# Moving the last residual load of a streaming RMSNorm into SyncE's queue, between the last x groups

## The chip, the cores and the metric

One NeuronCore of a Trainium2 chip. The metric is device time in microseconds; fast means within 1.5% of the quickest run of the same kernel. Repeated runs of one kernel agree within about half a microsecond to one and a half, at most 1.8 us (nine runs of the kernel before in one job). A profiled span is some 1.8 us shorter than the timed run that it comes from, so spans are compared with spans and times with times.

## The reference

```python
# x, residual: (32, 2048, 2048) float32; gamma: (2048,); eps = 1e-6
z = x + residual
rms = np.sqrt(np.mean(z ** 2, axis=-1, keepdims=True) + eps)
return (z / rms * gamma).astype(np.float32)
```

65,536 rows of 2048 numbers are read twice (x and residual) and written once: 1.61 GB.

## The kernel before

Rows are cut into 65 tiles, 0 to 64. Tile 0 has three rows in each of 128 partitions, tile 64 five, the others eight. Two z buffers take x and become the output in place; one residual buffer `r_area` of nine rows is shared by neighbouring tiles, shifted so that the next residual can be loaded as soon as the first part of the tile before has been added. VectorE adds and scales, ScalarE squares and takes roots, SyncE issues x and the stores, ScalarE issues the residuals.

```python
def sp_turn(sp, i):                       # SyncE, tile i
    def load(q):                          # a quarter of the partitions of tile i+1
        sp.wait_ge(s_out[q], i * U)       # the same quarter of tile i-1 is stored
        load_x(sp, i + 1, q)
    Turn(i).wait(sp, "done", -1)          # tile i-1 is scaled
    for q in range(Q):                    # Q = 4
        store(sp, i - 1, q)
    for q in range(Q):
        load(q)
...
def act_turn(s, t, chain):                # ScalarE, tile i
    ...
    t.wait(s, "add_a")                    # first part of the tile is added
    squares(s, chain, z[p], a, m, ssq[p][0], 0)
    if i == last - 1:
        load_r(s, t, 1)                   # the last residual, on ScalarE's queue
    elif i:
        t.wait(s, "add_b")
        load_r(s, t, 1)
    ...
# SyncE after its turns: tile 63 in two stores, tile 64 in three (2, 2 and 1 rows)
sp.wait_ge(half, 1);                 store_rows(sp, last - 1, a0, b0)
Turn(last).wait(sp, "done", -1);     store_rows(sp, last - 1, a1, b1)
for k, (a, b) in enumerate(tail):
    sp.wait_ge(tail_ev["done"], k + 1)
    store_rows(sp, last, a, b)
```

Of the kernel before, what the change touches and what calls it, by code (L numbers as in the profile page):

```python
# [9 lines left out]
def kernel(  # L10
# [32 lines left out]
    Q = 4  # L43
# [9 lines left out]
    last = n_tiles - 1  # L53
# [6 lines left out]
    def rows(t, i):  # L60
        k = sizes[i]
        return t[starts[i] : starts[i] + P * k, :].rearrange("(p r) m -> p r m", r=k)
# [45 lines left out]
    def res(i, a, b):  # L108

        if i == 0:  # L110
            return z[0][:, 5 + a : 5 + b, :]
        e = 4 if i == last else 0 if i % 2 else 1
        return r_area[:, e + a : e + b, :]

    def parts(i):

        if i == 0:
            return [(0, 1), (1, 2), (2, 3)]
        return [(4, R), (1, 4), (0, 1)] if i % 2 else [(0, 4), (4, R - 1), (R - 1, R)]
# [21 lines left out]
    def inc(ins, kind, i):  # L141
        return ins.then_inc(ev[kind][i % 2], U)
# [5 lines left out]
    def load_x(sp, i, q):  # L148
        sp.dma_start(out=z[i % 2][group(q), : sizes[i], :], in_=rows(x_f, i)[group(q)]).then_inc(
            ev["x_in"][i % 2], U  # L150
        )
# [6 lines left out]
    def load_r(eng, t, d=0):  # L158
        i = t.i + d
        inc(  # L160
            eng.dma_start(  # L161
                out=res(i, 0, sizes[i]),
                in_=rows(r_f, i) if t.it is None else r_full[t.it + (i - 1)],
            ),
            "r_in",
            i,
        )

    def store(sp, i, q):
        sp.dma_start(out=rows(o_f, i)[group(q)], in_=z[i % 2][group(q), : sizes[i], :]).then_inc(  # L170
            s_out[q], U
        )
# [4 lines left out]
    def sp_turn(sp, i):  # L177


        def load(q):  # L180
            sp.wait_ge(s_out[q], i * U)
            load_x(sp, i + 1, q)

        Turn(i).wait(sp, "done", -1)
        for q in range(Q):
            store(sp, i - 1, q)
        for q in range(Q):
            load(q)


# [48 lines left out]
    def squares(s, chain, src, a, b, sq, c):  # L239

        for g in range(a, b):
            chain.wait()
            chain.next(
                s.activation(  # L244
                    out=sq_junk[:, :],
                    in_=src[:, g, :],
                    func=Act.Square,
                    accum_out=sq[:, c + g - a : c + g - a + 1],
                )
            )  # L250

    def root(s, chain, sq, rm):
        chain.wait()
        return s.activation(out=rm, in_=sq, func=Act.Sqrt, bias=eps_tile[:, :], scale=inv_d)  # L254

    def act_turn(s, t, chain):
        i, p = t.i, t.p
        (a, b), (a1, b1), (a2, b2) = parts(i)
        m = b - 1 if i else b
        t.wait(s, "add_a")  # L260
        squares(s, chain, z[p], a, m, ssq[p][0], 0)
        if i == last - 1:

            load_r(s, t, 1)
        elif i:
            t.wait(s, "add_b")
            load_r(s, t, 1)
        squares(s, chain, z[p], m, b, ssq[p][0], m - a)
        n = b - a
        inc(root(s, chain, ssq[p][0][:, :n], rms[p][0][:, :n]), "rms_a", i)  # L270
        c = min(a1, a2)
        n = b1 - a1 + b2 - a2
        if i == 0 or i == last - 1:
            t.wait(s, "add_b")
        squares(s, chain, z[p], a1, b1, ssq[p][1], a1 - c)
        t.wait(s, "add_c")
        squares(s, chain, z[p], a2, b2, ssq[p][1], a2 - c)
        inc(root(s, chain, ssq[p][1][:, :n], rms[p][1][:, :n]), "rms_b", i)
# [5 lines left out]
    def sync_program(sp):  # L284
        whole_x(sp, 0)
        load_r(sp, Turn(0))

        sp.wait_ge(tail_ev["add"], 1)
        for q in range(4):
            sp.dma_start(  # L290
                out=stage[32 * q : 32 * q + 1],
                in_=gamma.partition_broadcast(1).rearrange("p (a b) -> p a b", a=16),
            ).then_inc(g_in, U)
        load_r(sp, Turn(1))
        whole_x(sp, 1)
        for i in range(1, last):
            sp_turn(sp, i)
        (a0, b0), (a1, b1) = halves(last - 1)
        sp.wait_ge(half, 1)
        store_rows(sp, last - 1, a0, b0)  # L300
        Turn(last).wait(sp, "done", -1)
        store_rows(sp, last - 1, a1, b1)
# [3 lines that stand above are left out]
# [30 lines left out]
    def scalar_program(s):  # L336
        chain = Chain(s, act)
        for i in range(LO):
            act_turn(s, Turn(i), chain)
        with s.Fori(0, 2 * (n_iter - 1), 2) as it:  # L340
            n = chain.n
            chain.base = it * R
            for i in range(LO, LO + 2):
                act_turn(s, Turn(i, it), chain)
            assert chain.n - n == 2 * R
        chain.base = None
        chain.n = n + 2 * R * (n_iter - 1)
        for i in range(HI - 2, last):
            act_turn(s, Turn(i), chain)
        for k, (a, b) in enumerate(tail):  # L350
            s.wait_ge(tail_ev["add"], k + 2)
            squares(s, chain, z[last % 2], a, b, tail_ssq, a)
            root(s, chain, tail_ssq[:, a:b], tail_rms[:, a:b]).then_inc(tail_ev["rms"], 1)
# [46 lines left out]
```

## Time and profile before

| | kernel before |
|---|---|
| time, median of 4 (lowest to highest) | 3732.35 us (3732.1 to 3732.79) |
| busy: VectorE, ScalarE | 62%, 28% |
| DMA queues q1 and q10, share of 16 engines | 67.3% and 32.6% |
| last residual: issued, landed | 3666.60, 3692.2 us |
| last x group: issued, landed | 3676.59, 3698.07 us |
| span | 3730.9 us |

The two shares of the DMA queues add up to 99.9%, so the kernel moves bytes all the time.

### The profile page before, as it was taken

What the parts mean: (1) busy time and instruction counts of PE and PEld (TensorE: products, weight loads), DVE (VectorE), ACT (ScalarE), POOL (GpSimd) and SP (SyncE); (2) the same over time, 40 slices, a digit from 0 to 9 for tenths busy, and PEclk for the clock granted to TensorE, in tenths of its full rate; (3) what the DMA queues carried; (4) which work ended last, traced back from release to release, by engine and by line L of the source; (5) the groups of instructions that cost most, each with busy time, mean ns of one, the idle gap of its engine ahead of it and who ended that gap; (6) DMA issues with size and microseconds to landing.
All of it is one profiled execution on the core that took longest, in us unless ns stands there. A gap on an engine that the chain in (4) does not pass through costs nothing.

```text
span 3730.9 us, 4005 instructions
## 1 busy us (share of the span) xinstructions
DVE 2300.7 (62%) x842; ACT 1059.7 (28%) x1157; POOL 0.2 (0%) x4
## 2 busy tenths in 40 slices
DVE  5657566575665756657556575565755657556566
ACT  2323233232331322313223132231322313223132
POOL 0000000000000000000000000000000000000000
DMA  9999999999999999999999999999999999999998
GB/s 421 433 436 429 436 432 433 437 430 437 430 436 436 431 436 430 436 433 433 437 430 436 433 433 437 430 436 431 434 436 430 438 430 436 434 432 429 435 429 377
DMA packets 34695, 1610.73 MB, mean 432 GB/s; under 512 B 9281, under 2 KB 9345, under 8 KB 9345
## 3 DMA queue, kind: packets, MB, share of 16 engines
q1 hardware_dynamic: 25616, 1085.34, 67.3%
q10 hardware_dynamic: 9072, 525.34, 32.6%
q14 instruction: 7, 0.05, 0.0%
HBM read 1073.77 MB, written 536.87 MB: 432 GB/s over the span
## 4 chain that ended last, share of the span: by engine, by line
DMA 65%; DVE 27%; issue 5%; SPq 1%; ACT 1%; another core or an unknown queue 1%; ACTq 0%; DVEq 0%
DMA out_dram<-z 33%; DMA z<-in_x_dram 30%; DVE z L193 13%; DVE z L198 13%; SPq L170 1%; DMA r_area<-in_residual_dram 1%; ACT sq_junk L244 0%; DMA z<-in_gamma_dram 0%; ACTq L161 0%; DVE rstd L217 0%; ACT rms L254 0%; DVEq L314 0%; DVEq L139 0%; SPq L290 0%
## 5 line engine op out<-in xcount | busy, mean ns | idle before, releaser
L193 DVE TENSOR_TENSOR z<-z,r_area 128x8192 f32<-128x8192 f32 (+2 forms) x192 | 1104.8, 5810 | 1339.8 <-DMA z<-in_x_dram 1325.1
L244 ACT ACTIVATE sq_junk<-z 128x2048 f32<-128x2048 f32 x512 | 962.1, 1879 | 2640.9 <-DVE z L193 2630.7
L198 DVE SCALAR_TENSOR_TENSOR z<-z,rstd,gamma_tile 128x2048 f32<-128x2048 f32 x507 | 1156.5, 2344 | 4.5
L244 ACT ACTIVATION_READ_ACCUMULATOR sq_junk<-z 128x1 f32 x512 | 95.4, 186 | 0.0
L217 DVE RECIPROCAL rstd<-rms 128x4 f32<-128x4 f32 (+1 forms) x128 | 22.4, 175 | 58.2 <-ACT rms L254 58.2
L254 ACT ACTIVATE rms<-ssq,eps_tile 128x4 f32<-128x4 f32 (+1 forms) x128 | 38.0, 297 | 11.7
L198 DVE SCALAR_TENSOR_TENSOR z<-z,tail_rstd,gamma_tile 128x2048 f32<-128x2048 f32 x5 | 11.6, 2346 | 0.1
L311 DVE LOAD_MASK_SELECT gamma_tile<-z x1 | 0.0, 14 | 16.2 <-DMA z<-in_gamma_dram 16.2
L193 DVE TENSOR_TENSOR z<-z 128x2048 f32<-128x2048 f32 x3 | 6.7, 2284 | 0.0
L311 DVE STREAM_SHUFFLE gamma_tile<-z 128x2048 f32<-128x2048 f32 x1 | 2.3, 2290 | 0.0
L309 DVE MEMSET z<- 128x2048 f32 x1 | 1.8, 1765 | 0.4 <-issue 0.4
L244 ACT ACT_TABLE_LOAD x1 | 1.3, 1283 | 0.9 <-SPq L80 0.9
L254 ACT ACT_TABLE_LOAD x1 | 1.3, 1283 | 0.1
L254 ACT ACTIVATE tail_rms<-tail_ssq,eps_tile 128x2 f32<-128x2 f32 (+1 forms) x3 | 0.9, 295 | 0.1
L308 DVE MEMSET eps_tile<- 128x1 f32 x1 | 0.1, 59 | 1.0 <-SPq L80 1.0
L327 DVE RECIPROCAL tail_rstd<-tail_rms 128x2 f32<-128x2 f32 (+1 forms) x3 | 0.5, 158 | 0.0
L381 POOL MEMSET const-bfloat16-1.0<- 128x1 bf16 x1 | 0.1, 101 | 0.0
L381 POOL MEMSET const-uint8-127<- 128x1 uint8 x1 | 0.1, 101 | 0.0
L381 POOL MEMSET const-float32-0.0<- 128x1 f32 x1 | 0.1, 98 | 0.2 <-issue 0.2
L381 POOL MEMSET const-float32-1.0<- 128x1 f32 x1 | 0.1, 98 | 0.0
## 6 DMA issues: line engine op xcount, KB each, us to landing
out_dram<-z SPq DMA_DIRECT2D x2, 4096.0 KB, 27.5
z<-in_x_dram SPq DMA_DIRECT2D x4, 1280.0 KB
r_area<-in_residual_dram ACTq DMA_DIRECT2D x1, 5120.0 KB, 25.6
out_dram<-z SPq DMA_DIRECT2D x2, 2048.0 KB, 8.7
z<-in_x_dram SPq DMA_DIRECT2D x249
out_dram<-z SPq DMA_DIRECT2D x248, 30.6
z<-in_x_dram SPq DMA_DIRECT2D x1, 3072.0 KB
z<-in_residual_dram SPq DMA_DIRECT2D x1, 3072.0 KB, 17.2
```

Of the source, the lines that this page charges most:

```text
L170: sp.dma_start(out=rows(o_f, i)[group(q)], in_=z[i % 2][group(q), : sizes[i], :]).then_inc(s_out[q], U)
L193: return v.tensor_add(out=s, in0=s, in1=res(i, a, b))
L198: ins = v.scalar_tensor_tensor(out=s, in0=s, scalar=rs[:, c + g - a : c + g - a + 1], in1=gamma_tile[:, :], op0=mult, op1=mult,)
L217: v.reciprocal(out=rstd[p][h][:, :n], in_=rms[p][h][:, :n]).then_inc(dve, U)
L244: s.activation(out=sq_junk[:, :], in_=src[:, g, :], func=Act.Square, accum_out=sq[:, c + g - a : c + g - a + 1],)
L254: return s.activation(out=rm, in_=sq, func=Act.Sqrt, bias=eps_tile[:, :], scale=inv_d)
L308: v.memset(eps_tile[:, :], float(eps))
L309: v.memset(stage, 0.0).then_inc(tail_ev["add"], 1)
L311: v.stream_shuffle(gamma_tile[:, :].rearrange("p (a b) -> p a b", a=16), stage, [0] * 32)
L327: v.reciprocal(out=tail_rstd[:, a:b], in_=tail_rms[:, a:b]).then_inc(dve, U)
L381: nc = _bacc.Bacc("TRN2", target_bir_lowering=False, num_devices=1)
```

## The change

Its intent seems to be to bring the last residual in ahead of everything that is written afterwards, in one queue with the x groups: SyncE waits for the first addition of tile 63 and issues the residual of tile 64 between the second and the third x group. ScalarE no longer issues it.

```diff
         for q in range(Q):
+            if i == last - 1 and q == Q // 2:
+                Turn(i).wait(sp, "add_a")
+                load_r(sp, Turn(i), 1)
             load(q)
...
-        if i == last - 1:
-            load_r(s, t, 1)
-        elif i:
+        if 0 < i < last - 1:
             t.wait(s, "add_b")
             load_r(s, t, 1)
```

## The prediction

> **What bounds the kernel now.** I read the page of the kernel before from the top: its span, the share of each engine, the 40 slices, the queues, and the chain that ended last.
>
> ```profile
> span 3730.9 us, 4005 instructions
> DVE 2300.7 (62%) x842; ACT 1059.7 (28%) x1157; POOL 0.2 (0%) x4
> ...
> DMA  9999999999999999999999999999999999999998
> ...
> q1 hardware_dynamic: 25616, 1085.34, 67.3%
> q10 hardware_dynamic: 9072, 525.34, 32.6%
> ...
> HBM read 1073.77 MB, written 536.87 MB: 432 GB/s over the span
> ```
>
> No compute engine is above 62%, while the DMA row is at nine tenths or more in 39 slices of 40. The two queues together fill 67.3 + 32.6 = 99.9% of the time of the 16 DMA engines. q1 is SyncE's queue (x and the stores), q10 ScalarE's (the residuals: 525 MB is all of the residual but the first tile and the next). So the time is the bytes over the rate: 1610.7 MB / 432 GB/s = 3728 us. The change moves no byte away. It can only work at the end, where the last residual is loaded, and so the rest of the reading is in the last 80 us. The timeline of that stretch:
>
> ```profile
> 3653.80 17.36 DVE L193 TENSOR_TENSOR z<-z,r_area 128x8192 f32<-128x8192 f32 x3 [21.38 <-DMA z<-in_x_dram]
> 3658.60 18.46 SPq L149 DMA_DIRECT2D z<-in_x_dram  x4
> 3662.52 1.88 ACT L244 ACTIVATE sq_junk<-z 128x2048 f32<-128x2048 f32 x1 [40.35 <-DVE z L193]
> ...
> 3666.60 0.33 ACTq L161 DMA_DIRECT2D r_area<-in_residual_dram  x1
> ...
> 3680.48 40.82 SPq L175 DMA_DIRECT2D out_dram<-z  x5
> ...
> 3698.09 10.96 DVE L193 TENSOR_TENSOR z<-z,r_area 128x4096 f32<-128x4096 f32 x3 [8.39 <-DMA z<-in_x_dram]
> ```
>
> Number the tiles 0 to 64. At 3653.80 tile 63 is there and its first addition starts; it is done at 3662.5, where ScalarE's square starts. The four x groups of tile 64 are issued from 3658.60 to 3677.06, each behind the store of the same group of tile 62. The last residual is issued at 3666.60 by ScalarE. The first store of tile 63 is issued at 3680.48, and the last tile's additions start at 3698.09, released by x and not by the residual. The chain in order of time ends with the same pieces:
>
> ```profile
> 3634.26 42.31 DMA out_dram<-z
> 3676.57 0.02 issue
> 3676.59 21.48 DMA z<-in_x_dram
> 3698.07 0.02 issue
> 3698.09 8.88 DVE z L193 x3
> ```
>
> From there the chain runs over VectorE to the last store. That is one true path, but I think it is not the only one, and the table by stretches says why (columns: the stretch, its length, DVE, ACT and POOL busy, clock, DMA share, GB/s):
>
> ```profile
> 3658.00:3698.00 40.00, 31.63 (x13) 16.50 (x18) 0.00 (x0) 1.00 0.98 408
> 3698.00:3710.00 12.00, 11.87 (x5) 7.35 (x8) 0.00 (x0) 1.00 0.83 358
> 3710.00:3714.00 4.00, 3.96 (x4) 3.40 (x6) 0.00 (x0) 1.00 0.06 25
> 3714.00:3731.00 17.00, 6.91 (x4) 0.00 (x0) 0.00 (x0) 1.00 0.74 312
> ```
>
> Between 3710 and 3714 the 16 engines are 6% busy: 25 GB/s is what one engine moves (432 / 16 = 27 GB/s). One engine still stores tile 63 while fifteen have run dry. The same shows once more at the end: in the DMA view from 3727 on, a few packets come one after the other at 14 GB/s on the mean. So **one DMA engine lags**, and what it still has to move sets the end. A check: when x has landed (3698.07) that engine has a sixteenth of tile 63's two stores left (8.39 MB / 16 = 0.524 MB) and of the last tile's three (5.24 MB / 16 = 0.328 MB). 0.852 MB / 27 GB/s = 31.6 us, which gives 3729.6; the span ends at 3730.9, the difference being the last store's landing. And backwards: from 3653.80, when x of tile 63 has landed, to 3698.07 it has a sixteenth of tile 62's stores (8.39 MB), of x (5.24 MB) and of the residual (5.24 MB): 18.87 MB / 432 GB/s = 43.7 us, against 44.3 in the trace. So this engine had no gap of more than about half a microsecond for the last 77 us.
>
> **What the Trainium skill says.** The page "DMA: Bandwidth & Descriptors", section "Issuing engines are not separate DMA queues", says that DMAs begun by ScalarE and SyncE run on the same 16 engines and interleave, and that a second issuer saves only issue time. The trace agrees: the shares of q1 and q10 sum to 99.9% and not more. Its section "Queues, rings and completion order" says that each DMA engine takes the descriptors of one ring in order, and turns between the queues that have work, a packet at a time. The DMA view from 3668 to 3692, when the residual was in flight, shows this: q10 took 53.6% and q1 45.4% of the engines, 99.0% together. The page "Perfetto Trace Analysis", section "DMA Instruction — HWDGE (DVE, Sync)", says that an issue row covers the generation of descriptors and not the moving; here an issue takes 0.33 us (the residual) while its landing is 25.6 us away.
>
> **The change, part by part.**
> 1. Removed from ScalarE: one issue, 0.33 us beside a square that was running (a square starts at 3666.59, the issue at 3666.60). Its sums of squares end before VectorE needs them: VectorE's additions end at 3671.16 and ScalarE's root of 0.30 us begins at 3670.72. Worth 0.
> 2. Added to SyncE: a wait for tile 63's first addition, and the same issue. The wait is met at 3662.5, before the second x group is issued (3663.42), so it costs nothing; the residual is issued at about 3664.0, 2.6 us earlier than before. The third group waits for the store of its group (3668.30 before), so the issue's 0.33 us lies in SyncE's waiting time. Worth 0.
> 3. Moved: the residual's 5.24 MB from q10 to q1, behind the rest of tile 62's stores and x groups 0 and 1, in front of x groups 2 and 3 and of tile 63's stores. Tile 62's last store no longer shares the engines with it, so it lands earlier: 3676.57 becomes some 3670 to 3673, and the last x group is issued as much earlier. It gains no time by that: on the lagging engine the residual is now all ahead of it in the ring. Before, the residual landed at 3666.60 + 25.6 = 3692.2, so it too had been moved wholly before x landed. In both orders the lagging engine must do stores, x and residual, 18.87 MB / 16, before the last x group is there. Worth 0: landing at 3697 to 3698.5.
> 4. Tile 63's stores are issued when VectorE has scaled, 3680.48 and about 3689.7. Nothing before that waits for the residual. They are behind the reads in q1 in both kernels. Worth 0.
> 5. The last tile: first additions at the later of x and residual, still x. First tail store issued about 15.7 us later (3713.8), when the lagging engine still has stores up to 3698.07 + 0.524 MB / 27 GB/s = 3717.5. So 3.7 us of slack stay, and VectorE's tail is not the bound.
>
> The sum is 0. What is left is a microsecond of sharing: the 40 us in which the reads lie ran at 408 GB/s where the steady state (3632 to 3658) shows 436, so up to some 2.5 us on the average engine depend on how packets of the two queues and the waits fall. Most of that is the fifteen fast engines waiting for groups that the slow one holds back, and costs nothing.
>
> **The rivals.**
> (a) *A gain, because the last x group no longer shares the engines with the residual.* For it: it took 21.48 us to land, and the residual landed 5.9 us before it. If x and the residual could both be there when the residual was (3692.2), the end would be up to 5 us earlier, 3727. Against: the bytes are the same, and the engines were 98% busy while they moved. The gap of 5.9 us is x of the same ring, not idleness.
> (b) *A gain, because the reads go in front of tile 63's stores.* This seems to be the intent. For it: the residual overlapped with the store issued at 3680.48. Against: the store lies behind the last x group in the same ring, so on the lagging engine it had not begun; on the others it only filled time that they had to spare. At most 1 to 2 us.
> (c) *A loss, because one queue hides less than two.* For it: 3658 to 3668, with q1 alone, shows 389 GB/s, and 3668 to 3692 with both 411. Against: 3692 to 3698, q1 alone, shows 430 at 99.6%. If the residual ran 5% slower, 5.24 MB / 408 GB/s = 12.8 us would grow by 0.6 us.
> (d) *A new wait on SyncE.* If the first addition came later than the second store group, groups 2 and 3 would be held. In the trace 0.9 us are to spare, and a ring with two store groups and two x groups has some 10 us of work. Worth 0 even if it waits.
>
> **Range and chances.** The middle is 3732.23 less a few tenths for the packets that no longer turn between two queues: 3731.9. (b) with its 2 us gives the lower side; (c) and (d), and the scatter of 0.4 us in the times before, the upper. I take 3729.5 to 3734.0. Two per cent are 75 us, more than the whole part that the change touches, and no rival comes near: within 2% at 0.99.
>
> **What would show it.** The residual's issue in SyncE's row near 3664, and none in ScalarE's; q10 down by 5.24 MB and q1 up by as much; the last store of tile 62 landing some 4 to 6 us earlier, and yet the last x group within 1 us of 3698; VectorE's last additions released by x; tile 63's stores still issued at 3680.5; the 4 us of 25 GB/s still there. The prediction is wrong if the last additions start before 3696, which would say that the lagging engine had gaps that I don't see, or if SyncE is held at the new wait for long enough to empty its ring.

## The result, and the profile after

The changed kernel takes 3732.68 us (median of 4, 3732.09 to 3732.86) against 3732.35 us (3732.1 to 3732.79). The ratio is 1.0, its 95% interval 0.9983 to 1.0018. Ratios here are the mean time of one kernel's fast runs over that of the other's of the same rounds, so not quite the ratio of the medians. The interval is about 6.5 us wide to each side; what is said below of single microseconds rests on the small scatter of the runs and on the traces, not on it. A second measurement, in a later job, gave 3732.8 against 3732.5 us. The change is worth nothing that can be told from zero; if anything it costs 0.3 us.

The page of the changed kernel, its span and the two queues' packets, MB and share:

```profile
span 3731.1 us, 4005 instructions
...
q1 hardware_dynamic: 25760, 1090.58, 67.7%
q10 hardware_dynamic: 8928, 520.10, 32.2%
```

The 5.24 MB have moved from q10 to q1, and the sum of shares is the same 99.9%. The timeline of the end:

```profile
3653.79 17.36 DVE L197 TENSOR_TENSOR z<-z,r_area 128x8192 f32<-128x8192 f32 x3 [21.38 <-DMA z<-in_x_dram]
3658.59 5.35 SPq L149 DMA_DIRECT2D z<-in_x_dram  x2
3663.98 0.60 SPq L161 DMA_DIRECT2D r_area<-in_residual_dram  x1
3668.29 5.36 SPq L149 DMA_DIRECT2D z<-in_x_dram  x2
...
3698.26 10.96 DVE L197 TENSOR_TENSOR z<-z,r_area 128x4096 f32<-128x4096 f32 x3 [8.57 <-DMA z<-in_x_dram]
```

The residual now stands between two pairs of x groups, and SyncE did not stall for it. The last additions start at 3698.26 instead of 3698.09, still released by x. The chain of waits shows the one thing that did move:

```profile
3634.25 38.91 DMA out_dram<-z
3673.16 0.02 issue
3673.18 25.06 DMA z<-in_x_dram
3698.24 0.02 issue
```

The last store of tile 62 landed 3.4 us earlier (3673.16, not 3676.57), so the last x group was issued 3.4 us earlier. It then took 25.06 us to land instead of 21.48, 3.6 us longer, and came at the same moment. **Waiting in one place became waiting in another.** The table by stretches (stretch, length, DVE, ACT and POOL busy, clock, DMA share, GB/s) is also as before:

```profile
3658.00:3698.00 40.00, 31.62 (x13) 16.51 (x18) 0.00 (x0) 1.00 0.98 407
...
3710.00:3714.00 4.00, 4.00 (x3) 3.57 (x6) 0.00 (x0) 1.00 0.08 33
```

The dip to little more than one engine's rate between 3710 and 3714 is still there. The lag can also be seen directly. A transfer counts as landed when its semaphore (a counter that other engines wait on) has had sixteen increments, and the trace has the time of each. For the first group's store of tile 62, in the kernel before and after alike, fifteen had come by 3651.8 and the sixteenth at 3658.6. That the late one belongs to the same DMA engine each time is inferred; the increments carry no engine. The lag is not there from the start: in the 14 traces it was 0.1 to 2.0 us on this group's store of tile 24 and 6.5 to 7.7 us on that of tile 62, and in between it grew by some 0.15 us for most tiles of 58 us (and by 0.9 at tiles 40 and 56). If it is one engine, it is a little slower than the others, and what is seen at the end has built up. For the very last store of the kernel, fifteen came from 3727.5 to 3727.6 and the sixteenth at 3729.9 in the changed kernel (3727.3 to 3727.5 and 3729.7 before). So two paths end close together: fifteen engines that were dry and begin when VectorE releases the first tail store, and one engine that never was and ends 2.3 us later.

### The profile page after: what moved, and what is told of

It reads as the page before. It is cut to its first block, busy times and chain, and to the rows that moved or that the text cites. A ratio compares the mean times of both kernels' runs of the same rounds, so it can differ in the third digit from the quotient of the medians.

```text
span 3731.1 us, 4005 instructions
## 1 busy us (share of the span) xinstructions
DVE 2300.6 (62%) x842; ACT 1059.7 (28%) x1157; POOL 0.2 (0%) x4
## 4 chain that ended last, share of the span: by engine, by line
DMA 65%; DVE 27%; issue 5%; SPq 1%; ACT 1%; another core or an unknown queue 1%; ACTq 0%; DVEq 0%
DMA out_dram<-z 33%; DMA z<-in_x_dram 31%; DVE z L197 13%; DVE z L202 13%; SPq L170 1%; DMA r_area<-in_residual_dram 1%; ACT sq_junk L248 0%; DMA z<-in_gamma_dram 0%; ACTq L161 0%; DVE rstd L221 0%; ACT rms L258 0%; DVEq L315 0%; DVEq L139 0%; SPq L291 0%
## 5 line engine op out<-in xcount | busy, mean ns | idle before, releaser
L312 DVE LOAD_MASK_SELECT gamma_tile<-z x1 | 0.0, 14 | 16.5 <-DMA z<-in_gamma_dram 16.5
```

What stands on the lines that cost most here:

```text
L312: v.stream_shuffle(gamma_tile[:, :].rearrange("p (a b) -> p a b", a=16), stage, [0] * 32)
```

## The experiments

Every experiment is an edit of the changed kernel, but act_at_once (and its second look, act_again) is one of the kernel before. The spread of the times is small, but tile 63 starts up to 0.9 us earlier or later from one trace to the next, so the table also counts from the start of tile 63's additions in the same trace: until the first scaling of tile 64 (a), and until the end of the span (b). Times are medians of five runs, of four for the two kernels' first rows; the kernel before in the same jobs had 3732.41, 3732.56 and 3732.50 us. For two jobs both are given. The interval of the ratio to the kernel before leaves out 1 for delay4, one_row, behind_store and tail_15 alone.

| kernel | time, us | (a) us | (b) us |
|---|---|---|---|
| before | 3732.35 | 55.4 | 77.1 |
| changed | 3732.68; 3732.80 | 55.5; 55.4 | 77.3; 77.2 |
| delay1 | 3733.08 | 57.4 | 77.1 |
| delay4 | 3739.07 | 64.5 | 84.0 |
| one_row | 3722.21 | 46.9 | 67.0 |
| behind_store | 3741.89 | 66.7 | 86.2 |
| hold_half | 3736.78 | 59.6 | 81.2 |
| hold_add_c | 3733.42 | 56.1 | 77.8 |
| x_first | 3733.99; 3733.87 | 56.5; 56.1 | 78.2; 77.8 |
| act_at_once | 3732.16; 3732.26 | 54.7; 54.7 | 76.4; 76.4 |
| tail_15 | 3741.81 | 55.9 | 86.2 |

The theory: one DMA engine lags behind the others and its ring (its own list of transfers that wait in a queue) is never empty, so its bytes set the end. The main rival: the chain that the profile prints, over VectorE, is the only path.

### Is VectorE's tail the bound? delay1 and delay4

```diff
         t.wait(v, "r_in")
+        for g in range(1):          # 4 in delay4
+            v.memset(r_area[:, g, :], 0.0)
```

Rows 0 to 3 of the residual buffer are free at that point, so the result stays right.

> The changed kernel with one VectorE memset of 128x2048 (about 1.77 us by the memset row of before) between the arrival of the last tile and its additions, so the whole tail on VectorE and ScalarE slides by 1.8 us. Lagging-engine theory: the first tail store's first packet slides from about 3714.8 to 3716.6, still before the lagging engine has finished tile 63's stores at 3717.3, so the time stays within 0.5 us of the changed kernel. Rival, that the chain over VectorE is the only path to the end: +1.8 us.

> The same with four memsets, 7.1 us. Lagging-engine theory: the first tail store's packets come at about 3721.9, the lagging engine is dry from 3717.3, so +4.6 us (7.1 less the 2.5 us of slack). Rival, chain over VectorE alone: +7.1 us.

delay1: the first scaling came 1.9 us later (a), the end not at all (b: 77.1 against 77.3); the time is 3733.08 us against 3732.68, and the scatters overlap. That delay was hidden; fifteen increments of the last store now came only 0.2 us before the sixteenth. In delay4 the memsets took 1.76 us each with 0.38 us between them, and the last x group landed 0.5 us later, so the tail slid by 9.0 us in all, more than the 7.1 that was expected; the time rose by 6.4 us (4.6 were expected for the shorter delay) and (b) by 6.7. The rival would have it rise by the whole 9.0. The difference, 2.3 us, is the slack, and it is the 2.3 us by which the sixteenth engine came after the fifteen. Stretches of delay4 show where the delay began to count:

```profile
3698.00:3717.00 19.00, 16.56 (x7) 5.12 (x6) 0.00 (x0) 1.00 0.58 248
3717.00:3723.50 6.50, 6.43 (x6) 5.63 (x8) 0.00 (x0) 1.00 0.00 0
```

and the same second stretch of the changed kernel:

```profile
3717.00:3723.50 6.50, 4.07 (x3) 0.00 (x0) 0.00 (x0) 1.00 1.00 426
```

In delay4 all sixteen engines, the lagging one too, are dry until the first tail store comes; in the changed kernel they store at full rate. So neither path is the only one: VectorE's is 2.3 us shorter than that of the lagging engine.

### Is the residual hidden beside x? one_row

```diff
-                load_r(sp, Turn(i), 1)
+                inc(sp.dma_start(out=res(last, 0, 1),
+                                 in_=rows(r_f, last)[:, 0:1, :]), "r_in", last)
```

> The changed kernel, but the last residual load brings one of its five rows (1.05 MB instead of 5.24 MB); the result is wrong in the last tile on purpose. Lagging-engine theory: 4.19 MB / 432 GB/s = 9.7 us less, the last additions start near 3689.7 (VectorE is busy with tile 63 until then), the span ends near 3721.4. Rival, that the residual is hidden beside x because only x is waited for: 0 to -1 us.

The result was wrong (relative error 0.09), the time 3722.21 us: 10.5 us less, where the bytes left out were worth 9.7 by the rate. So the residual is not hidden although VectorE's last wait is for x: x waits behind it. The last additions:

```profile
3689.26 10.96 DVE L201 TENSOR_TENSOR z<-z,r_area 128x4096 f32<-128x4096 f32 x3
```

There is no idle time in front of them any more; VectorE comes straight from scaling tile 63. With less to read, the engine that computes had become the bound of that moment.

### Does the order in the ring count at all? behind_store, x_first, act_at_once

behind_store takes the two new lines out of the loop and issues the residual after the first store of tile 63:

```diff
         store_rows(sp, last - 1, a0, b0)
+        load_r(sp, Turn(last - 1), 1)
```

> The changed kernel, but the residual goes through SyncE's queue behind the first store of tile 63 (issued after 3680.5). Lagging-engine theory: the residual lands at about 3698.2 + 9.7 (that store is now in front of it) = 3708, the last additions start about 10 us later and are released by the residual; the first tail store's packets come at about 3724.9 while the lagging engine is dry from 3717.3, so +7.6 us. Rival, that only the sum of bytes counts and their order never: 0.

3741.89 us, 9.2 us more than the changed kernel. 7.6 were expected; the last additions slid by 11.1 us instead of 10, and the last tile's read packets were longer here, 1.67 us on the mean instead of 1.61. The last additions are now released by the residual:

```profile
3709.53 10.96 DVE L193 TENSOR_TENSOR z<-z,r_area 128x4096 f32<-128x4096 f32 x3 [19.68 <-DMA r_area<-in_residual_dram]
```

and afterwards the engines have nothing to do for a while:

```profile
3718.80:3726.00 7.20, 7.13 (x6) 6.02 (x8) 0.00 (x0) 1.00 0.00 0
3726.00:3740.00 14.00, 6.35 (x4) 0.00 (x0) 0.00 (x0) 1.00 0.89 375
```

Being in front of the stores that follow is therefore worth 9.2 us, but the kernel before had that already: its residual was issued 14 us ahead of the first of them. (a) grew by 11.1 us and (b) by 8.9; the difference, 2.2 us, is again about the slack.

x_first keeps it in front of the stores but behind all four x groups, and act_at_once gives it back to ScalarE, right after the first addition and before any square:

```diff
         for q in range(Q):
             load(q)
+        if i == last - 1:                 # x_first, SyncE
+            Turn(i).wait(sp, "add_a")
+            load_r(sp, Turn(i), 1)
...
         t.wait(s, "add_a")
+        if i == last - 1:                 # act_at_once, ScalarE
+            load_r(s, t, 1)
         squares(s, chain, z[p], a, m, ssq[p][0], 0)
```

> The changed kernel, but the residual goes behind all four x groups in SyncE's queue, still in front of tile 63's stores. Lagging-engine theory: the same bytes lie ahead of the last additions, so they start within 0.5 us of 3698.3, now released by the residual instead of x, and the time stays within 0.5 us. Rival, that the place between the x groups counts: a difference of 2 us or more.

> The residual on ScalarE's queue as in the kernel before, but issued as soon as the first addition is done (about 3662.6 instead of 3666.6). It parts the queue from the time of issue. Lagging-engine theory: 0 within 0.5 us, last additions near 3698. Rival, that an earlier issue gains and one queue gives it back: about -1 us or more against both kernels.

x_first took 3733.99 us, 1.4 us above the kernel before in that job, where the theory allowed 0.5: a miss, though short of the rival's 2 us. Its trace shows the exchange that the theory speaks of: x landed at 3685.0 and the residual at 3698.8, where the changed kernel has the residual at 3692.2 and x at 3698.24. act_at_once took 3732.16, 0.4 below. As the changed kernel had been timed in another job, the three were taken again on one chip:

> The changed kernel again, on the same chip as the next three, so that differences of a microsecond can be read. Lagging-engine theory: within 0.5 us of the kernel before. If the order of the reads is worth a microsecond, as one run each of x first (+1.4 us on before) and ScalarE at once (-0.4 us) hint, the changed kernel stands between these two.

> The residual behind all four x groups, beside the changed kernel on one chip. If the microsecond of the first look is real: +1 us on the changed kernel, with the read packets of the last tile slower on the mean; if it was the other job's chip: within 0.5 us.

> The residual on ScalarE's queue as soon as the first addition is done, beside the changed kernel on one chip. If the first look is real: -0.5 us on the changed kernel; otherwise within 0.3 us.

On one chip: act_at_once 3732.26 (3731.73 to 3733.07), changed 3732.80 (3732.36 to 3733.34), x_first 3733.87 us (3733.26 to 3734.23). x_first is 1.4 us above the kernel before in both jobs, and 1.1 us above the changed kernel, whose scatter it touches. act_at_once is half a microsecond quicker than the changed kernel, and its last additions start 0.8 us earlier in both of its traces (43.6 us after tile 63's, against 44.4 and 44.5), but its times overlap with those of both kernels. So it is no version that clearly beats them.

The packet records of the trace give a hint where the microsecond lies. The last tile's reads are 256 packets of 40,960 bytes, 16 for each engine. Their mean duration was 1.53 and 1.54 us in act_at_once, 1.59 in the kernel before, 1.61 in the changed one (both traces), 1.67 and 1.68 in x_first. Times 16 that is 24.6, 25.4, 25.7 and 26.8 us: the same order as the times. But these are means over all sixteen engines, the records don't name the engine, and one order of reads scatters too: delay1, delay4 and tail_15, which read as the changed kernel does, had means of 1.59, 1.63 and 1.63 us. So before and changed cannot be told apart by them. What bears on the lagging engine alone is the time between the landing of tile 62's last store and that of the last read, in kernels with all these transfers in one queue: 24.9 to 25.5 us in the five traces of the changed order, 25.9 and 25.6 in x_first, which is just outside. act_at_once, with two queues, has its last x group 43.6 us after tile 63's start, against 44.3 to 44.9 in those five, and 44.3 in the kernel before. Two stretches of x_first, in which its engines move less, and of the changed kernel below:

```profile
3668.00:3682.00 14.00, 13.93 (x9) 10.76 (x14) 0.00 (x0) 1.00 0.91 356
...
3690.00:3698.00 8.00, 0.00 (x0) 0.00 (x0) 0.00 (x0) 1.00 0.90 389
```

```profile
3668.00:3682.00 14.00, 13.93 (x9) 11.08 (x14) 0.00 (x0) 1.00 0.98 423
...
3690.00:3698.00 8.00, 0.00 (x0) 0.00 (x0) 0.00 (x0) 1.00 1.01 436
```

The first stretch is fifteen engines waiting for the residual that SyncE issues at 3673.39; by the theory that alone would cost nothing. The longer packets go with the later landing; that they cause it is not shown. Why packets grow (up to 3.0 us instead of 1.51 in the changed kernel, mostly when the reads begin and just before the stores follow) no run here settles.

### Does the new wait on SyncE cost? hold_add_c and hold_half

```diff
-                Turn(i).wait(sp, "add_a")      # met at 3662.5
+                Turn(i).wait(sp, "add_c")      # hold_add_c: met at 3671.2
+                sp.wait_ge(half, 1)            # hold_half instead: met at 3680.4
```

> The changed kernel, with SyncE's new wait on tile 63's third addition (done at about 3671.2) in place of its first (3662.5). The lagging engine has work in its ring until about 3678.7, so 0 within 0.5 us. Rival, that any wait on SyncE delays the last x groups and so the end: 3671.2 less 3664.0, +7 us.

> The changed kernel, but SyncE waits for the first scaled half of tile 63 (about 3680.4) where it now waits for the first addition (met at 3662.5), before it issues the residual and x groups 2 and 3. Lagging-engine theory: that engine has the rest of tile 62's stores until 3672.7 and x groups 0 and 1 (4 packets of 1.5 us) until 3678.7; the residual's first packet comes near 3681.7, so a gap of about 3 us and +3 us in the time. Rival, that the wait on SyncE counts in full: 3680.4 less 3664.0, +16 us.

hold_add_c: counted from tile 63's start, the residual was issued 7.2 us later than in the changed kernel (3671.64 - 3654.25 = 17.4 us against 3663.98 - 3653.79 = 10.2), and the time was 3733.42 us, 0.6 above the changed kernel of the same job, with scatters that overlap. Nearly all of a wait of 7 us was hidden. hold_half held SyncE 16.5 us longer (26.7 us after tile 63's start), and the time rose by 4.1 us, where 3 were expected and the rival said 16. Its stretches:

```profile
3668.00:3682.00 14.00, 13.93 (x9) 11.29 (x14) 0.00 (x0) 1.00 0.29 103
3682.00:3690.00 8.00, 7.90 (x4) 0.00 (x0) 0.00 (x0) 1.00 0.86 369
```

Fifteen engines stood still for most of the first stretch and only the lagging one still moved; it ran dry too at the end, which is the part that cost time. At the very end of hold_half the fifteenth and the sixteenth increment came together, at 3734.1: **the pause had let the fifteen lose their lead, and the lag was gone.** The fourth microsecond goes with longer read packets (mean 1.67 us, times 16 another 1 us by the mean of all engines); that they cause it is not shown.

### Taking work off the lagging engine: tail_15

```diff
-            store_rows(sp, last, a, b)
+            for c, e in ((0, 120), (120, 128)):
+                sp.dma_start(out=rows(o_f, last)[c:e, a:b, :],
+                             in_=z[last % 2][c:e, a:b, :]).then_inc(s_tail, U)
```

The kernel's final wait then counts six stores instead of three.

> The changed kernel, but each of the last tile's three stores is cut into partitions 0 to 119 and 120 to 127. If the split over DMA engines follows the count of partitions, 120 go over 15 engines and 8 over 8, so one engine gets nothing of the last 5.24 MB (12 us of its work). Lagging-engine theory, if that engine is the lagging one: it ends at 3717.3 and the others, which were 7 us ahead, set the end, so -3 to -4 us, the first version below both kernels. If the lagging engine is another one: +0.8 to +1.6 us. Rival, that no single engine lags and VectorE's tail sets the end: 0 to +1 us.

3741.81 us: 9.1 us slower, which no theory had said. The last additions were where they were; the stores themselves were slow:

```profile
3714.00:3726.00 12.00, 7.45 (x6) 0.05 (x1) 0.00 (x0) 1.00 0.89 225
3726.00:3740.00 14.00, 0.00 (x0) 0.00 (x0) 0.00 (x0) 1.00 0.55 188
```

and SyncE's row for the six stores (start, length):

```profile
3714.38 14.03 SPq L307 DMA_DIRECT2D out_dram<-z  x6
```

The changed kernel moves 403 GB/s from 3714 to 3726. The 256 packets of 16,384 bytes took 0.97 us on the mean instead of 0.62. SyncE was held too: the issues took 0.33 to 4.28 us each, where the changed kernel's three took 0.33, and the last began at 3726.2 instead of 3721.1. The split itself was as expected: the six stores made 75 increments, which is 15 and 8 for each pair and one more for each store. The experiment says nothing about which engine lags, since the cut by partitions made every store worse; whether the packets or the issues came first, and why, is open. It is an inconclusive run, and by the increments of the last store the most that evening out the engines could have brought is 2.3 us, 0.06%.

## Why the prediction was right or wrong

The predicted time was 3731.9 us with a range of 3729.5 to 3734.0, within 2% at 0.99; it was 3732.68 us. It was right, and as far as the experiments go for its reason: the last x group lands when the lagging engine has moved stores, x and residual, in whatever order but for about a microsecond. The number alone tests little, for any theory in which the change is worth about 0 would have met it; the landings and the experiments are the test.

1. *ScalarE's issue, worth 0*: so it was. VectorE's first scaling of tile 63 began at 3671.32, before the change at 3671.33.
2. *SyncE's wait and issue, worth 0*: the issue was at 3663.98, as foreseen, but took 0.60 us and not ScalarE's 0.33. The third x group came at the same moment as before, so this cost nothing. hold_add_c and hold_half show that some 7 us more would have been nearly free, and that the wait counts where the lagging engine's ring empties.
3. *The bytes only change queue, landing at 3697 to 3698.5*: 3698.24. The last store of tile 62 came 3.4 us earlier, a little less than the 4 to 6 us named in the list of signs. one_row (10.5 us for bytes worth 9.7) and x_first (x and residual exchange places) show that the bytes in front of x, and not what is waited for, set its landing.
4. *The stores of tile 63 unmoved*: issued at 3680.47, before at 3680.48. behind_store shows that rival (b) named a real effect, worth 9.2 us, which the kernel before had already taken.
5. *VectorE's tail has 3.7 us of slack*: the sign is right, the size is not. The term took the issue of the first tail store (3713.8) where its first packets count, which the packet records have 0.8 us later, at 3714.6 (3714.8 in the changed kernel). The slack was 2.3 us by delay4 and by the increments. It did not matter here.

The one step that nothing bears out is the middle of the range: "less a few tenths for the packets that no longer turn between two queues". The mean packet was 1.59 us before and 1.61 after, and the time rose by 0.3 us, both inside the scatter, so neither this gain nor rival (c), a loss in one queue of about 0.6 us, is shown. act_at_once, with two queues and an early issue, has the shortest packets and speaks for (c) rather than for the gain.

Three readings in the prediction are not right, and none carries the result. Rival (d) gives two store groups and two x groups "some 10 us of work"; they are 6.81 MB, 15.8 us at 432 GB/s, which fits the 7 us of hold_add_c that cost almost nothing. The shares of q10 and q1 from 3668 to 3692 show that both queues moved at once, but not that an engine turns between them packet by packet or keeps the order of a ring (the landings of x_first bear out the order). And the 1.3 us between 3729.6 and the end of the span are not the last store's landing: its last increment came at 3729.7.

Rival (a) fell: no idle time lay between the residual's landing and x's.

## What to carry to other kernels

When the DMA engines are full, ask what the slowest of the sixteen still has in its ring, and in front of what; changing the order of reads that are all needed at once moved waits about here, and between the best and the worst order lay 1.6 us of 3732. Test it by cutting bytes (it helps although nobody waits for them) and by delaying the compute chain by a known amount (what the end does not follow is the slack). Being in front of later stores is worth real time, so check first whether the transfer isn't there already.

## What the Trainium skill lacked or had wrong

- "DMA: Bandwidth & Descriptors", section "Issuing engines are not separate DMA queues", holds here: moving 5.24 MB from one issuer to the other changed the time by 0.3 us of 3732. What it lacks is that the order in which reads stand may have a small price of its own: the same 256 read packets took 1.53 to 1.68 us on the mean in four orders (1.59 to 1.63 in five traces of one order), and the times differed by 1.6 us on one chip.
- The same page, table of "Latency and other measured facts", tells of DMA engines that are usually slower, and its best guess puts it down to rings that only GpSimd's path has. This kernel issues no DMA from GpSimd, and one engine still lagged by 6.8 us behind the fifteenth on tile 62's stores and by 2.3 us on the last, having fallen back by some 0.15 us for most tiles. The trace does not name the engine.
- The same page, section "Why a DMA increments its semaphore by 16 and not by 1", tells how the count of partitions chooses the number of engines, and the 75 increments of tail_15 agree; but no page tells what an uneven cut costs: with 120 and 8 partitions instead of 128, packets of 16,384 bytes took 0.97 us instead of 0.62, and issues on SyncE up to 4.28 us instead of 0.33.
- "Perfetto Trace Analysis", section "DMA Instruction — HWDGE (DVE, Sync)", gives no duration for an issue, and "SBUF — State Buffer" only "a few hundred ns" for setting up a transfer: the same load's issue took 0.33 us on ScalarE, on SyncE 0.43 to 0.60 us when it followed another issue closely, and 0.34 us when it did not.
